# The first stage of a two-layer backbone step: a new order of steps, adaLN sums of two column blocks, weights and small vectors laid out by the host

## The chip, the cores and the metric

The kernel runs on one core of one Trainium2 chip. The metric is the device time of one launch in microseconds (us). Five engines work in parallel, each through its own instructions in order: TensorE (PE; its weight loads are listed apart as PEld), VectorE (DVE), ScalarE (ACT), GpSimd (POOL) and SyncE (SP), which here only issues DMA transfers. Engines wait for one another by semaphores.

## The reference

One inference step of a hybrid backbone with two layers, on 1024 latent ("sample") tokens and 256 context ("prompt") tokens of width 1024. What the first stage computes is the normalised and modulated input of layer 0, and the first of the projections behind it:

```
sh_p, sc_p, gt_p = _adaln(c_ctx[None, :], w_mod[l], b_mod[l])     # from silu(c) @ w_mod + b_mod
sh_s, sc_s, gt_s = _adaln(c, w_mod[l], b_mod[l])
hp = _rmsnorm(yp, norm_g[l]) * (1.0 + sc_p) + sh_p
hs = _rmsnorm(ys, norm_g[l]) * (1.0 + sc_s) + sh_s
...
qa, ka, va, za, qb, kb, vb, ob, zb, gb = jnp.split(h @ w_in, AB_SPLITS, axis=-1)
```

Layer 0 then runs windowed attention and a bidirectional matrix memory side by side, layer 1 latent attention; each ends in an output projection, a gate and a residual. All is float32 in and out. Products are made from pairs of rounded float32 parts, high and low, with three matmuls each (high by high, high by low, low by high).

## The kernel before

Tokens lie in three chunks: 0 and 1 of 512 sample tokens each, 2 of 256 prompt tokens. The input is ten tiles of 128 tokens by 1024, and the width is cut into KD = 8 column blocks k of 128.

The first stage is written out by hand: the text `STARTUP` is a list of steps, each a name with one or two digits, and `Startup.run` calls the method of that name. Each engine and each DMA queue gets its instructions in this order. No planner moves them. The steps are:

- `X t` loads token tile t (512 KB) and `W k i` a block of the adaLN weights: 1024 rows by 128 columns of the shift (i = 0) or the scale (i = 1), 512 KB, read in pieces of 512 B. Both take one of ten buffers `xin`. `F a` loads 256 rows by 256 columns of the first projection's weights into one of two buffers `wf` (256 KB). All go through SyncE's queue.
- `sq`, `xr`, `pw`, `sc`: sum of squares of a tile on ScalarE, its mean plus epsilon on VectorE, the power -0.5 on GpSimd, and the scaling of the tile by it (GpSimd for tiles 2, 4 and 6, VectorE for the others).
- `Ta`, `Tb`: four transposes each on TensorE; `ea`, `eb`: the copies out of PSUM into `xT` (ScalarE for a, VectorE for b).
- `M k`: the adaLN sums of column block k, 16 matmuls with the condition vectors as the stationary operand (32 records in the profile); `e`: their scaling by 0.5 on ScalarE; `C`: a transpose; `A`: four small VectorE operations, which leave the scale A and the shift B of block k.
- `t ci k`: xT times A plus B, on VectorE (line 370); `h`: its high part, on ScalarE (line 373); `l`: its low part, on VectorE or GpSimd (line 378).
- `c k`, `s k`: high part on ScalarE (line 362) and low part on GpSimd (line 366) of the projection's weights.
- `pa ci k`: for both units (two groups of 128 output columns) of chunk ci, the two products with the high part of the activations; `pb ci k`: the one with the low part. A wide product has 512 columns (chunks 0 and 1), a narrow one 256 (chunk 2). A unit adds up 24 of them in one PSUM bank, and then its `done` runs: a copy out of PSUM (line 1558), and a convolution over tokens with a gate (lines 1573 to 1583).

Ahead of the list, `setup_consts` and `setup_cond` load the constants and small vectors through ScalarE's queue; the vectors come as rows, and TensorE turns them into columns. Behind the list stand the loads (`after.ask`) and splits (`after.split`, lines 522 and 523) of the next block's weights, the block of attention values (272 columns, units of 24 matmuls for each tile of 128 tokens), and the products of chunk 2. The splits stand in the queues behind the convolutions, in this order:

```
after.ask()
after.ask()
for ci in range(2):
    start.pa(ci, KD - 1)
    start.pb(ci, KD - 1)
    after.split()
    after.ask()
for k in range(KD):
    start.pa(2, k)
    start.pb(2, k)
    if k in (1, 3):
        after.split()
```

After it come the values block, the gates of the matrix memory (a long chain of small VectorE operations, in `gates`) woven with the next projection, and all the rest.

Of the kernel before, what the change touches and what calls it, by code (L numbers as in the profile page):

```python
# [19 lines left out]
D = 1024  # L20
# [12 lines left out]
X0 X1 X2 sq0 X3 sq1 xr0 pw0 X4 sc0 sq2 xr1 Tb0 pw1 sq3 X5 xr2 Ta0 pw2 sc1 sc2 ea0 eb0 Tb1 W00 sq4 xr3  # L33
Ta1 eb1 pw3 Tb2 sq5 xr4 W01 sc3 pw4 Ta2 sc4 eb2 ea1 Tb3 X6 ea2 xr5 Ta3 eb3 ea3 pw5 Tb4 M0 X7 sc5 eb4 Ta4
e0 sq6 Tb5 W10 C0 eb5 Ta5 ea4 A0 W11 sq7 xr6 pw6 t00 sc6 ea5 F0 xr7 h00 W20 l00 pw7 M1 sc7 c1 W21 Tb6 c0
s1 Ta6 e1 eb6 Tb7 ea6 s0 Ta7 eb7 F1 C1 ea7 pb00 A1 W30 pa00 t10 M2 c3 t01 W31 c2 s3 h10 t11 s2 e2 pa10
h01 W40 l10 h11 C2 pa01 A2 W41 l01 M3 l11 t12 pa11 e3 F2 t02 h12 C3 X8 pb11 h02 l12 A3 M4 l02 c5 X9 pa02
c4 s5 t03 e4 C4 s4 t13 pa12 sq8 W50 pb02 A4 h03 pb10 xr8 t04 pw8 pb01 W51 sq9 pa03 l03 t14 h13 sc8 pb12
W60 h14 pa13 xr9 l13 pw9 h04 Tb8 l14 W61 sc9 M5 eb8 Tb9 e5 l04 F3 Ta9 C5 W70 ea9 eb9 Ta8 pb13 ea8 A5 M6
c7 W71 t23 c6 s7 pa04 t05 e6 h23 s6 t15 h05 C6 pb04 l23 A6 pa14 h15 l05 t25 M7 t16 h25 l25 pa15 t24 e7  # L40
h16 t06 C7 h24 pb05 l16 h06 A7 pa16 t22 pa06 l24 t07 h22 t17 l22 pb16 h07 pa05 t27 h17 l07 t20 pb14 h27
l17 pb03 h20 l27 t21 l20 t26 h21 l15 h26 l21 l06 l26 pb15 pb06
# [161 lines left out]
def setup_consts(K):  # L204
    nc, c = K.nc, K.const
    small = c.tile([128, 6, 128], F32, tag="small", name="small")
    K.dma_act(small, K.I["k_small"].rearrange("p (a f) -> p a f", a=6))
    K.small = small
    K.ident = small[:, 0, :]
    K.mbf = c.tile([128, 3, 128], BF16, tag="mbf", name="mbf")  # L210
    nc.vector.tensor_copy(K.mbf[:, 0, :], small[:, 0, :])
    nc.vector.tensor_copy(K.mbf[:, 1:3, :], small[:, 4:6, :])
# [9 lines left out]
def setup_cond(K, sp):  # L222
    nc, c = K.nc, K.const
    K.condT = c.tile([128, 16], F32, tag="condT", name="condT")
    crow = sp.tile([16, 128], F32, tag="crow", name="crow")
    cth = sp.tile([16, 128], F32, tag="cth", name="cth")
    K.dma_act(crow[0:8, :], K.I["c"].rearrange("a (k p) -> (a k) p", p=128))
    K.dma_act(crow[8:16, :], K.I["c_ctx"].rearrange("(k p) -> k p", p=128))
    nc.scalar.activation(cth, crow, AF.Tanh, scale=0.5)
    nc.vector.scalar_tensor_tensor(crow, cth, 1.0, crow, ALU.add, ALU.mult)  # L230
    ps = K.ps()
    K.tr(ps[:, 0:16], crow)
    nc.vector.tensor_copy(K.condT, ps[:, 0:16])

    grow = sp.tile([16, 128], F32, tag="grow", name="grow")
    K.dma_act(grow, K.I["norm_g"].rearrange("l (k p) -> (l k) p", p=128))
    K.gcol = c.tile([128, 16], F32, tag="gcol", name="gcol")
    ps = K.ps()
    K.tr(ps[:, 0:16], grow)
    nc.vector.tensor_copy(K.gcol, ps[:, 0:16])  # L240
    brow = sp.tile([16, 128], F32, tag="brow", name="brow")
    K.dma_act(brow, K.I["b_mod"][0, 0:2 * D].rearrange("(k p) -> k p", p=128))
    K.bcol = sp.tile([128, 16], F32, tag="bcol", name="bcol")
    ps = K.ps()
    K.tr(ps[:, 0:16], brow)
    nc.vector.tensor_copy(K.bcol[:, 0:8], ps[:, 0:8])
    nc.vector.tensor_scalar(K.bcol[:, 8:16], ps[:, 8:16], 1.0, None, ALU.add)
    cw = sp.tile([48, 128], F32, tag="cwr", name="cwr")
    K.dma_act(cw, K.I["conv_b"][0].rearrange("j (k p) -> (j k) p", p=128))
    K.cw = c.tile([128, 3, 16], F32, tag="cw", name="cw")  # L250
    ps = K.ps()
    K.tr(ps[:, 0:48], cw)
    pv = ps[:, 0:48].rearrange("p (j k) -> p j k", j=3)
    nc.vector.tensor_scalar(K.cw[:, :, 0:8], pv[:, :, 0:8], 0.5, None, ALU.mult)
    nc.vector.tensor_scalar(K.cw[:, :, 8:16], pv[:, :, 8:16], 1.0 / 32, None, ALU.mult)
    K.condP = cond_cols(K, sp)
    K.modd = [K.t(K.dram, [2, 3 * D], F32, f"modd{l}") for l in range(2)]
    K.A = [None, None]
    K.Bm = [None, None]


class Startup:


    def __init__(self, K, sp, first):
        self.K, self.sp, self.first = K, sp, first
        self.units = first.fn(first.w)
        first.w[:] = [None] * KD
        K.A[0], K.Bm[0] = [K.const.tile([128, 2, 8], F32, tag=f"{n}0", name=f"{n}0") for n in "AB"]
# [3 lines left out]
    def run(self, order):  # L273
        for token in order.split():
            name = token.rstrip("0123456789")
            getattr(self, name)(*[int(a) for a in token[len(name):]])
# [8 lines left out]
    def W(self, k, i):  # L285
        w = self.ws[k, i] = self.slot().rearrange("p (k f) -> p k f", k=KD)
        f = slice(i * D + k * 128, i * D + (k + 1) * 128)
        self.K.dma(w, self.K.I["w_mod"][0, :, f].rearrange("(k p) f -> p k f", p=128))

    def F(self, a):  # L290
        self.first.ask()
        self.wf[a] = self.first.wf.pop(0)

    def sq(self, t):
        ss = self.r[t] = self.K.t(self.sp, [128, 1], F32, "xss", 4)
# [3 lines left out]
    def xr(self, t):  # L299
        r = self.K.t(self.sp, [128, 1], F32, "xr", 4)  # L300
# [18 lines left out]
    def kept(self, t, a, copy):  # L319
        ci, i = chunk_of(t)  # L320
        copy(self.xT[ci][:, a:a + 4, i * 128:(i + 1) * 128], self.bank[t, a].rearrange("p (k t) -> p k t", k=4))
# [20 lines left out]
    def e(self, k):  # L342
        self.rows[k] = self.K.t(self.sp, [128, 128], F32, "mrow", 3)
        self.K.nc.scalar.mul(self.rows[k], self.bank[k][:, 0:128], 0.5)

    def C(self, k):
# [2119 lines left out]
```

## Time and profile before

| | |
|---|---|
| median of 3 runs | 2611.69 us (2610.7 to 2613.67) |
| the profiled execution's own time | 2613.18 us |
| its span, first to last instruction | 2611.4 us |
| mean granted TensorE clock | 0.992 |
| TensorE busy | 2541.8 us, 97% of the span |
| VectorE, ScalarE, GpSimd busy | 65%, 55%, 43% |
| first transposes of token tiles | 12.46 us |
| first product of the first block | 28.36 us |
| first matmul of the values block | 90.38 us |

The span is what the profile shows; the execution's own time has 1.8 us more around it. Of the rows shown further on: a row of instructions in order of time begins with its start and its duration, then engine, line, operation, tiles, shapes and count, and in brackets the idle time before it and what ended that. Rows of groups end with total busy time, mean duration in nanoseconds and the idle time before. A matmul's duration overlaps that of the next, so the pace is read from start to start. A row of waits has the total, the times and the longest.

### The profile page before, as it was taken

Reading aid. Unit: us, or ns where it says so; the run is one execution under the profiler, and the core shown is the slowest. Engines: PE = TensorE matmul, PEld = TensorE weight load, DVE = VectorE, ACT = ScalarE, POOL = GpSimd, SP = SyncE. Lnnn points to the kernel's source line nnn. Section 1 sums busy time; section 2 is a strip of 40 time slices with the busy share of each in tenths; the row PEclk is TensorE's granted clock in tenths of the full one; section 3 lists DMA queues with packets and bytes.
Section 4 is the critical chain, followed back from the end, with each engine's and each line's share of the span. In section 5 each row is a group of like instructions: output and inputs, shape, how many; then the busy total and the mean of one; then the engine's idle time right before and its main releaser. Section 6 shows DMA issues by size and latency. Waiting matters only on the chain.

```text
span 2611.4 us, 48697 instructions
## 1 busy us (share of the span) xinstructions
PE 2541.8 (97%) x16493; PEld 2253.4 (86%) x16493; DVE 1709.5 (65%) x3959; ACT 1438.4 (55%) x3660; POOL 1119.8 (43%) x1512
## 2 busy tenths in 40 slices
PE   7799999999999999999999999999999999999998
PEld 5789898898898888887888888898899999999887
DVE  7361565656647676577777546526888888888754
ACT  5332544544534433477666533234788888888842
POOL 5212333323224344356455453224455545555832
PEclk9899999999999999999999999999999999999999
DMA  8456576566666664445443454523311101101334
GB/s 242 154 177 187 164 198 194 163 199 188 176 200 207 211 212 145 140 145 154 134 124 109 131 192 134 159 73 101 87 32 32 44 27 38 36 27 30 119 99 131
DMA packets 352955, 347.21 MB, mean 133 GB/s; under 512 B 36065, under 2 KB 297886, under 8 KB 352450
## 3 DMA queue, kind: packets, MB, share of 16 engines
q1 hardware_dynamic: 352402, 343.65, 43.6%
q8 instruction: 131, 2.15, 0.4%
q14 instruction: 118, 0.97, 0.1%
q10 hardware_dynamic: 304, 0.44, 0.0%
HBM read 233.49 MB, written 110.50 MB: 132 GB/s over the span
## 4 chain that ended last, share of the span: by engine, by line
PE 84%; DVE 4%; DMA 4%; issue 3%; ACT 2%; POOL 2%; SPq 1%; ACTq 0%; POOLq 0%; DVEq 0%
PE mm L116 33%; PE S L116 29%; PE V L116 8%; PE T L120 6%; PE D L116 3%; PE mm L120 3%; SPq L151 1%; PE T L116 1%; DMA o_x<-y 1%; DMA att_q<-ql 0%; POOL wl L523 0%; DVE xT L370 0%; DMA caT<-csz 0%; POOL w L1022 0%; DMA w<-in_w_out_c 0%
## 5 line engine op out<-in xcount | busy, mean ns | idle before, releaser
L523 POOL TENSOR_TENSOR wl<-wf,wh 128x256 fp32r<-128x256 f32 (+3 forms) x280 | 223.4, 822 | 524.1 <-ACT wh L522 487.3
L116 PE MATMUL mm<-hTh,wh 128*128 128x512 f32 (+1 forms) x912 | 329.3, 361 | 0.9 <-DVE scr L769 0.9
L116 PE MATMUL mm<-hTl,wh 128*128 128x512 f32 (+1 forms) x912 | 324.6, 356 | 0.0
L116 PE MATMUL mm<-hTh,wl 128*128 128x512 f32 (+1 forms) x912 | 324.6, 356 | 0.0
L116 PE MATMUL S<-cK,cQ 96*128 96x512 f32 (+3 forms) x1248 | 301.0, 365 | 2.5 <-ACT cPa L2368 1.1
L2416 DVE TENSOR_TENSOR cpl<-T,cph 128x512 fp32r<-128x512 f32 x336 | 227.8, 685 | 38.2 <-ACT cph L2415 34.5
L116 PEld LDWEIGHTS S<-cK,cQ 96*128 96x128 f32 (+1 forms) x1248 | 192.6, 189 | 24.1 <-ACT cPa L2368 3.0
L2415 ACT CAST cph<-T 128x512 fp32r<-128x512 f32 x336 | 191.4, 589 | 29.1 <-PE T L120 16.8
L116 PEld LDWEIGHTS mm<-hTh,wl 128*128 128x128 f32 x912 | 171.4, 188 | 26.9
L116 PEld LDWEIGHTS mm<-hTh,wh 128*128 128x128 f32 x912 | 171.8, 188 | 23.9 <-DVE scr L769 1.1
L116 PEld LDWEIGHTS mm<-hTl,wh 128*128 128x128 f32 x912 | 171.9, 188 | 22.8
L2366 DVE TENSOR_REDUCE cmx<-S 128x1 f32<-128x512 f32 x256 | 173.2, 683 | 20.7 <-PE S L116 18.7
L116 PE MATMUL V<-cph,cV 128*128 128x256 f32 x672 | 177.1, 289 | 1.2 <-DVE co L2431 0.8
L116 PE MATMUL V<-cpl,cV 128*128 128x256 f32 x672 | 171.8, 284 | 0.8 <-DVE cst L2343 0.4
L1290 ACT CAST att_ph<-mm 128x512 fp32r<-128x512 f32 x168 | 98.5, 586 | 98.3 <-PE mm L120 96.5
L2347 POOL TENSOR_SCALAR cPa<-cPa,cst 128x512 f32<-128x512 f32 x128 | 98.7, 771 | 114.3 <-DVE cst L2344 93.3
L1291 DVE TENSOR_TENSOR att_pl<-mm,att_ph 128x512 fp32r<-128x512 f32 x168 | 115.8, 689 | 37.3 <-ACT att_ph L1290 32.1
L116 PE MATMUL mm<-wh,hTh 128*128 128x256 f32 x480 | 136.2, 284 | 4.1 <-DVE scr L1596 4.1
L116 PE MATMUL mm<-wl,hTh 128*128 128x256 f32 x480 | 135.4, 282 | 0.1
L116 PE MATMUL mm<-wh,hTl 128*128 128x256 f32 x480 | 135.3, 282 | 0.0
L116 PEld LDWEIGHTS V<-cph,cV 128*128 128x128 f32 x672 | 126.6, 188 | 8.3 <-DVE co L2431 1.4
L1279 POOL TENSOR_SCALAR att_p<-att_p,att_den 128x640 f32<-128x640 f32 (+1 forms) x128 | 97.4, 774 | 84.4 <-DVE att_den L1276 33.6
(472 smaller groups left out, 7772.1 us busy)
## 6 DMA issues: line engine op xcount, KB each, us to landing
wf<-in_w_in_ab SPq DMA_DIRECT2D x120, 256.0 KB
in<-in SPq DMA_DIRECT2D x40, 514.0 KB
in<-in SPq DMA_DIRECT2D x32, 386.0 KB
mw<-in_w_mod SPq DMA_DIRECT2D x48, 256.0 KB
in<-scr SPq DMA_DIRECT2D x40, 258.0 KB
o_x<-y SPq DMA_DIRECT2D x20, 512.0 KB
xin<-in_w_mod SPq DMA_DIRECT2D x16, 512.0 KB
in<-cx SPq DMA_DIRECT2D x32, 256.0 KB
```

The costliest lines, as they stand in the source:

```text
L116: return self.nc.tensor.matmul(out, lhsT, rhs, start=start, stop=stop)
L120: self.nc.tensor.transpose(out, in_, self.ident[:p, :p])
L151: self.nc.sync.dma_start(f(out), f(in_))
L523: K.nc.gpsimd.tensor_sub(wl, wf[:, k], wh.bitcast(F32))
L1279: nc.gpsimd.tensor_scalar(pv, pv, den[:, i:i + 1], 1.0, ALU.mult, ALU.mult)
L1290: K.nc.scalar.copy(ph, self.T)
L1291: K.nc.vector.tensor_sub(pl, self.T, ph.bitcast(F32))
L2347: nc.gpsimd.tensor_scalar(pv, pv, wt[:, c:c + 1], rd, ALU.mult, ALU.mult)
L2366: nc.vector.tensor_reduce(mx[:, b, c:c + 1], S, AX.X, ALU.max, negate=True)
L2415: nc.scalar.copy(ph, T_)
L2416: nc.vector.tensor_sub(pl, T_, ph.bitcast(F32))
```

## The change

- The list is new: 281 steps, with other orders of the tiles (6, 4, 2, 5, 3, 7, 0, 1, later 9 and 8) and of the column blocks. Steps that move or scale data have a letter for the engine: `a` ScalarE, `v` VectorE, `p` GpSimd (`ea4a`, `t13v`, `l01p`). The wide `t` run nine times on VectorE and seven on ScalarE, the narrow ones five and three times; the `l` run twelve times on VectorE and twelve on GpSimd; six tiles are scaled on GpSimd and four on VectorE; of the copies out of PSUM eleven run on ScalarE and nine on VectorE.
- `M q` sums column blocks 2q and 2q + 1 at once, from four W loads; `e`, `C` and `A` follow once for each q, and `A` has two VectorE operations.
- The host lays out `k_wmod` (16 blocks of 512 KB, one for each W, 4 KB in a row for each partition) and `k_cols` (the small vectors as columns). `LK` loads the constants and `LS` the columns, on SyncE's queue. `setup_cond`, with its loads on ScalarE's queue and its transposes, goes; three more small transposes behind the first stage go too.
- The list takes in what stood behind it: `f` (loads of the values block's weights), `d` (high parts, ScalarE), `u` (low parts), `P q` (the products of chunk 2 for two column blocks), `v ci j` (the copy out of PSUM of a unit of chunks 0 and 1) and `G` (buffers of the next stage). The convolutions run behind the list.
- One small ScalarE operation (`warm`) runs ahead of the list, and the buffers of the small vectors `xss` and `xr` go from 4 to 10.

```diff
 STARTUP = """
-X0 X1 X2 sq0 X3 sq1 xr0 pw0 X4 sc0 sq2 xr1 Tb0 pw1 sq3 X5 xr2 Ta0 pw2 sc1 sc2 ea0 eb0 Tb1 W00 sq4 xr3
...
-l17 pb03 h20 l27 t21 l20 t26 h21 l15 h26 l21 l06 l26 pb15 pb06
+X6 X4 X2 sq6 X5 sq4 xr6 pw6 X3 sc6p sq2 xr4 pw4 LK sq5 xr2 pw2 X7 sq3 xr5 sc4v pw5 LS Tb6 X0 sc5p sc2v Ta4
+eb6a Ta6 xr3 ea4a Tb2 X1 pw3 ea6v sq7 Tb5 eb2v sc3p Ta5 W10 Ta2 sq0 xr7 eb5v pw7 Tb3 W00 Tb4 sc7p sq1 xr0
+ea5v W11 pw0 Tb7 eb3a xr1 pw1 ea2a sc0v W01 cth Ta3 eb4a sc1v Ta7 eb7a Ta0 F0 ck ea3a Ta1 gc X9 ea7a ea0v M0
+W31 c0 ea1a e0v s0p C0 Tb0 W30 A0 sq9 Tb1 t00v W20 t10v h00 xr9 pa00 eb0v h10 W21 pw9 c1 l10v sc9p pa10 t11a
+X8 l00v t01a pb10 Tb9 h01 s1v F1 M1 h11 eb1v l01p W61 Ta9 e1v sq8 eb9v pb00 l11p W60 C1 pb01 A1 c2 pa11 c3
+xr8 W71 gw pw8 t02a s2v pb11 h02 pa01 sc8p t13v W70 ea9a t03v pa02 s3p h13 t12v F2 h03 Ta8 pa13 l02v ea8a F3
+l03p h12 W41 M3 t21v l13p t20v c5 pa12 t23a W50 l12v e3a c6 s5p C3 Tb8 c4 A3 W51 pa03 h23 s6p c7 t17v t07a
+pb03 s7p t06v W40 pb12 h07 pb02 t22v s4p h21 pb13 t16a eb8v pa07 l07p f0 h22 t27v h06 f1 M2 l22v h16 l06p
+t26a pb07 e2v h27 l21v C2 l23p h26 pa16 A2 h17 l26p t14v pa06 t25a t05a t04v l16p pb06 h14 pa17 t24v h05
+l17p l27v pa14 h20 l05v h04 pa05 h25 l04p t15a l25v pa04 l20v h15 l14v pb16 d3 l15p h24 pb05 d0 pb04 l24v d1
+pb14 u0v d2 pa15 G u3v v00 u2p u1v v01 pb17 f2 pb15 P0 f3 P1 d4 v11 u4p P2 d6 d5 d7 u5p v10 P3 u7v u6v
 """
...
     def W(self, k, i):
         w = self.ws[k, i] = self.slot().rearrange("p (k f) -> p k f", k=KD)
-        f = slice(i * D + k * 128, i * D + (k + 1) * 128)
-        self.K.dma(w, self.K.I["w_mod"][0, :, f].rearrange("(k p) f -> p k f", p=128))
+        self.K.dma(w, self.K.I["k_wmod"][i * KD + k].rearrange("p (k f) -> p k f", k=KD))
...
+    def M(self, q):
+        ps = self.bank[q] = self.K.psT()
         for j in range(KD):
             for i in range(2):
-                o = 64 * i + 32 * (j % 2)
-                self.K.mm(ps[o:o + 32, 0:128], self.K.condP[:, j, :], self.ws[k, i][:, j, :], j < 2, j >= KD - 2)
...
+                for k in range(2):
+                    o = 64 * i + 32 * k
+                    self.K.mm(ps[o:o + 32, 0:128], self.K.condP[:, j, :], self.ws[2 * q + k, i][:, j, :], j == 0, j == KD - 1)
...
+    def A(self, q):
+        nc, ks = self.K.nc, slice(2 * q, 2 * q + 2)
+        v = self.bank[q][:, 0:128].rearrange("p (i k r) -> p i k r", i=2, k=2)[:, :, :, 0:2]
+        b = self.cols[:, 32:48].rearrange("p (i k) -> p i k", i=2)[:, :, ks]
+        nc.vector.tensor_add(self.ab[:, :, ks], v, b.unsqueeze(3).to_broadcast([128, 2, 2, 2]))
+        a = self.ab[:, 1, ks]
+        nc.vector.tensor_mul(a, a, self.K.gcol[:, ks].unsqueeze(2).to_broadcast([128, 2, 2]))
...
+    def P(self, q):
+        for k in self.order[2 * q:2 * q + 2]:
+            self.pa(2, k)
+            self.pb(2, k)
+
+    def v(self, ci, j):
+        u = self.units[3 * j + ci]
+        u.done(u.ps)
+        self.kept.pop()()
...
     with K.tc.manual_schedule():
-        start.run(STARTUP)
...
-        for k in range(KD):
-            start.pa(2, k)
-            start.pb(2, k)
-            if k in (1, 3):
-                after.split()
+        start.run(STARTUP, room)
...
+def _layouts(inputs):
...
+    w = inputs["w_mod"][0, :, 0:2 * D].reshape(KD, 128, 2 * KD, 128)
+    return {"k_cols": np.ascontiguousarray(np.concatenate([a.reshape(-1, 128) for a in cols]).T),
+            "k_wmod": np.ascontiguousarray(w.transpose(2, 1, 0, 3)).reshape(2 * KD, 128, D)}
```

More of the change, by code (lines that the diff above doesn't have):

```diff
@@ L219, in setup_consts @@
     nc.vector.memset(K.mhalf, -0.5)
[L222 to L259, printed above, removed]
@@ L270, in __init__, with run @@
         self.x, self.r, self.ws, self.wf, self.bank, self.rows = {}, {}, {}, {}, {}, {}
         self.xT = [sp.tile([128, KD, N], F32, tag=f"xT{ci}", name=f"xT{ci}") for ci, (_, N) in enumerate(CHUNKS)]
-    def run(self, order):
-        for token in order.split():
-            name = token.rstrip("0123456789")
-            getattr(self, name)(*[int(a) for a in token[len(name):]])
+        warm = K.t(sp, [128, 1], F32, "warm", 1)
+        K.nc.scalar.activation(warm, K.mhalf, AF.Square)
+    def run(self, order, room):
+        K, nc = self.K, self.K.nc
+        self.G = room
+        self.by = dict(a=nc.scalar, v=nc.vector, p=nc.gpsimd)
+        K.flow = self
+        for token in order.split():
+            name, at, by = re.fullmatch(r"([A-Za-z]+)(\d*)([avp]?)", token).groups()
+            getattr(self, name)(*[int(a) for a in at], *by)
+        for u in self.units[2::3]:
+            u.done(u.ps)
+        while self.kept:
+            self.kept.pop(0)()
+        K.flow = None
+        small = K.small
+        nc.vector.tensor_copy(K.mbf[:, 0, :], small[:, 0, :])
+        nc.vector.tensor_copy(K.mbf[:, 1:3, :], small[:, 4:6, :])
@@ new lines, in later, with LK, LS, cth @@
+    def later(self, f, n):
+        self.kept.append(f)
+    def LK(self):
+        self.K.dma(self.K.small, self.K.I["k_small"].rearrange("p (a f) -> p a f", a=6))
+    def LS(self):
+        self.K.dma(self.cols, self.K.I["k_cols"][:, 0:96])
+    def cth(self):
+        self.th = self.K.t(self.sp, [128, 16], F32, "cth", 1)
+        self.K.nc.scalar.activation(self.th, self.cols[:, 0:16], AF.Tanh, scale=0.5)
+    def ck(self):
+        K = self.K
+        K.nc.vector.scalar_tensor_tensor(K.condT, self.th, 1.0, self.cols[:, 0:16], ALU.add, ALU.mult)
+        K.condP = cond_cols(K, self.sp)
@@ new lines, in cast, with low, s @@
+    def cast(self, b, k):
+        b.w[k] = [self.K.t(b.wp, [128, b.width], F32R, n, int(2 * b.bufs))[:, 0:sum(n for _, n in b.cols)] for n in ("wh", "wl")]
+        self.K.nc.scalar.copy(b.w[k][0], self.wf[b, k // 2][:, k % 2])
+    def low(self, b, k, by):
+        wh, wl = b.w[k]
+        self.by[by].tensor_sub(wl, self.wf[b, k // 2][:, k % 2], wh.bitcast(F32))
+    def c(self, k):
+        self.order.append(k)
+        self.cast(self.first, k)
+    def s(self, k, by):
+        self.low(self.first, k, by)
@@ L827, in layer_ab, with room @@
     dense = Dense(blocks)
-    start = Startup(K, sp, blocks.pop(0))
-    after = blocks[0]
-    K.set_psum(S=4, T=4)
-    with K.tc.manual_schedule():
-        start.run(STARTUP)
+    start = Startup(K, sp, blocks.pop(0), blocks[0])
+    def room():
+        nonlocal gp, tp
         sp.release()
@@ L836, in layer_ab @@
         K.cvp = right("conv")
-        after.ask()
-        after.ask()
-        for ci in range(2):
-            start.pa(ci, KD - 1)
-            start.pb(ci, KD - 1)
-            after.split()
-            after.ask()
-        for k in range(KD):
-            start.pa(2, k)
-            start.pb(2, k)
-            if k in (1, 3):
-                after.split()
+    gp = tp = None
+    K.set_psum(S=4, T=4)
+    with K.tc.manual_schedule():
+        start.run(STARTUP, room)
     K.set_psum(S=6, T=2)
```

160 lines of the change are left out of this document (81 added, 79 removed).

## The prediction

> **What bounds the kernel now.** I read the page first, for the span and the slices; then TensorE's waits in the first 131 us; then the busy time by stage; then the chain that ended last where the longest wait ends; last TensorE's instructions in order of time, for the price of one matmul of each kind. The page and the waits:
>
> ```profile
> span 2611.4 us, 48697 instructions
> ...
> PE   7799999999999999999999999999999999999998
> ```
>
> ```profile
> PE S L116 <- ACT scr L1558: 13.4, 1, 13.4
> ...
> PE S L116 <- DVE hTl L378: 3.3, 1, 3.3
> ```
>
> TensorE is busy nine tenths and more of nearly every slice; its free time lies in the first two slices, of 65 us each, and those are the stage that the change rewrites. By stage (length; busy time of TensorE, its weight loads, VectorE, ScalarE, GpSimd; granted clock, DMA share, GB/s):
>
> ```profile
> 0.00:12.46 12.46, 1.02 (x5) 0.67 (x5) 3.28 (x18) 5.97 (x10) 2.71 (x8) 1.00 0.88 318
> ...
> 28.36:58.70 30.34, 29.24 (x295) 22.23 (x294) 27.65 (x60) 17.34 (x39) 19.87 (x20) 0.96 0.81 223
> 58.70:75.50 16.80, 13.47 (x68) 10.68 (x67) 12.23 (x24) 6.10 (x14) 9.69 (x14) 0.80 0.50 160
> 75.50:90.40 14.90, 0.22 (x2) 0.16 (x2) 5.58 (x16) 5.20 (x13) 3.69 (x5) 0.61 0.39 103
> 90.40:120.40 30.00, 30.00 (x219) 30.00 (x220) 7.43 (x25) 6.52 (x18) 4.38 (x6) 0.91 0.34 110
> ```
>
> TensorE does almost nothing until 12.46, is full from 28.36 with VectorE nearly full beside it, and from 75.50 to 90.40 has 0.22 us of work in 14.90. The wait that ends this hole is put down to a ScalarE copy, so I follow the chain there (start, length, what):
>
> ```profile
> 83.51 1.37 ACT wh L522 x4
> ...
> 84.91 0.77 POOL wl L523
> ...
> 85.69 0.37 SPq L151
> ...
> 86.12 3.10 DMA wf<-in_w_in_ab
> ...
> 89.64 0.41 ACT wh L522
> ...
> 90.38 41.68 PE S L116 x333
> ```
>
> The hole is the next block's weights: four casts, which in ScalarE's order stood behind convolution work and ran only at 83.51, a GpSimd subtraction that frees a staging buffer, a load, the cast of that load, and then the first matmul of the block of attention values at 90.38. After it TensorE runs for 41.68 us without a break. So what counts is when that block can start; a microsecond that it comes earlier is carried on by TensorE, which is the bound from there to the end.
>
> **What one thing costs.** TensorE in order of time, start and duration first:
>
> ```profile
> 19.20 1.08 PE L116 MATMUL T<-xin,condP 128*32 128x128 f32 x32
> 20.21 1.09 PE L120 MATMUL T<-small,xin 128*128 128x128 f32 x8
> 21.14 0.27 PE L120 MATMUL T<-small,mrow 128*128 128x128 f32 x1
> ...
> 28.36 1.20 PE L116 MATMUL S<-hTl,wh 128*128 128x512 f32 x2
> ...
> 40.09 1.54 PE L116 MATMUL S<-hTl,wh 128*128 128x512 f32 x6
> 41.46 0.40 PE L116 MATMUL S<-hTh,wh 128*128 128x512 f32 x1
> ...
> 69.40 0.39 PE L116 MATMUL S<-hTh,wh 128*128 128x256 f32 x1
> ...
> 74.94 0.40 PE L116 MATMUL S<-hTl,wh 128*128 128x256 f32 x2
> ...
> 90.38 0.59 PE L116 MATMUL S<-wh,hTh 128*128 128x272 f32 x1 [13.35 <-ACT scr L1558]
> ...
> 95.30 0.43 PE L116 MATMUL S<-wh,hTh 128*128 128x272 f32 x1
> ...
> 96.13 0.29 PE L116 MATMUL S<-wh,hTl 128*128 128x272 f32 x1
> ...
> 99.03 0.28 PE L116 MATMUL S<-wl,hTh 128*128 128x272 f32 x1
> ```
>
> From start to start: one adaLN sum of a column block (M, 32 records) 20.21 - 19.20 = 1.01 us; eight transposes 0.93, 0.116 each; six 512-wide matmuls 41.46 - 40.09 = 1.37, 0.228 each; the matmuls of 256 columns 46 steps in 74.94 - 69.40 = 5.54, 0.120 each. So the first stage holds, at full clock, 80 transposes 9.3, eight M 8.1, 96 wide products 21.9, 48 narrow ones 5.8 and some 0.4 of small transposes: 45.5 us.
>
> **The change, part by part.** Small vectors from the host: the six loads that ScalarE issued and four transposes with their copies go, and three more in the stages behind; one load of the columns (48 KB) and the constants go through SyncE's queue instead, ahead of the last X tiles. They add 0.44 MB there. The removed transposes lay before TensorE had anything else, or in the hole: nothing of their own.
>
> One M for two column blocks: as many matmuls (four times 64 records for eight times 32), while the scalings, transposes and the small VectorE work after them halve. That relieves VectorE, and makes a group of four W loads the unit that TensorE waits for.
>
> The adaLN weights' layout: each of the 16 W loads is one block of 4 KB a partition, as the X loads are, no longer 512 B pieces. The rate of X shows early, that of W with some F late:
>
> ```profile
> 7.00:12.00 5.00, 1.02 (x4) 0.64 (x4) 2.24 (x9) 4.93 (x9) 1.75 (x3) 1.00 1.03 379
> ...
> 42.00:47.00 5.00, 3.90 (x50) 3.02 (x49) 4.55 (x6) 2.02 (x6) 3.12 (x3) 1.00 0.97 264
> ```
>
> No run shows W in the new form. The ends are these rates, 379 and 264 GB/s, at a DMA share near 1.0 both times; I take 379, because the new form is that of X. The Trainium skill ("DMA: Bandwidth & Descriptors", Specifications) puts line rate at transfers of 512 B and more, by which W was there already and the layout would bring nothing. These rows, 264 in 512 B pieces beside 379, speak against it; the first rival is what it would make of the time.
>
> The order. Up to the first M the queue holds eight X, four W, constants and columns, 6.73 MB; with transfers from about 2 us on (the first row of the stage table: 318 GB/s over 12.46 us is 3.96 MB, 10.45 us at 379), they have landed at 2 + 6.73/0.379 = 19.8. M0 now sums two blocks, 2.0 us, to 21.8. Before, a first product took from 19.20 to 28.36, because other transposes stood in between; the chain itself is scaling, transpose, A, t and h:
>
> ```profile
> 20.37 0.28 ACT L344 ACTIVATE mrow<-T 128x128 f32<-128x128 f32 x1 [1.28 <-PE T L116]
> ...
> 23.57 0.63 ACT L373 CAST hTh<-xT 128x512 fp32r<-128x512 f32 x1
> ```
>
> ```profile
> 22.13 0.22 DVE L355 SCALAR_TENSOR_TENSOR B<-T,bcol,mhalf 128x2 f32<-128x2 f32 x1
> ...
> 22.78 0.56 DVE L370 TENSOR_SCALAR xT<-xT,A,B 128x512 f32<-128x512 f32 x1
> ...
> 29.46 3.37 DVE L370 TENSOR_SCALAR xT<-xT,A,B 128x512 f32<-128x512 f32 x3
> ```
>
> 0.3 for the scaling, 0.3 for the transpose, two VectorE operations 0.4, t 0.6, h 0.6, and 0.5 for the hand-overs: 2.7, so a first product at 24.5, 3.9 us earlier. Done by then are the transposes of eight X tiles (64, 7.4 us), M0 (2.0) and 0.1: 36.0 us of TensorE work are left, and the stage's last matmul would end at 60.5 if nothing stalled. What does stalling cost? Before, the work from 28.36 on was 96 wide and 48 narrow products, seven M, 17 transposes and the small ones, 21.9 + 5.8 + 7.1 + 2.0 + 0.8 = 37.6 us, and took 75.2 - 28.36 = 46.8: 9.2 lost, to the 3.3 us wait and to clocks of 0.96 and 0.80 above all. The new order's loss lies between 0 and 9.2; below 0 it can't go, as the work is counted at full clock. I take half, 4.6, since VectorE, which was nearly full, gives work away (nine wide t's for 16, five narrow for eight, six wide l's for eight, A's 32 operations become eight) and gets six narrow l's for none and five low parts of the next block, while ScalarE takes ten t's and eight casts. ScalarE has room for them:
>
> ```profile
> L297 ACT ACTIVATE xjk<-xin 128x1024 bf16<-128x1024 f32 x10 | 10.6, 1055 | 1.2 <-DMA xin<-in_x_prompt 1.1
> L373 ACT CAST hTh<-xT 128x512 fp32r<-128x512 f32 x16 | 9.4, 617 | 1.4 <-DVE xT L370 1.4
> L321 ACT COPY xT<-T 128x512 f32<-128x512 f32 x10 | 5.7, 582 | 7.1 <-PE T L120 7.1
> L373 ACT CAST hTh<-xT 128x256 fp32r<-128x256 f32 x8 | 3.2, 405 | 5.2 <-DVE xT L370 5.1
> L362 ACT CAST wh<-wf 128x256 fp32r<-128x256 f32 x8 | 2.9, 409 | 0.5 <-DMA wf<-in_w_in_ab 0.5
> ```
>
> squares 10.6, h's 9.4 and 3.2, eleven copies 6.4, ten t's at h's prices 5.5, 16 casts 6.5: 42 us in about 60. GpSimd does 12 l's for 16, six scalings for three and nine low parts for eight, so about what it did. Neither exceeds TensorE. The stage's last matmul then ends at 60.5 + 4.6 = 65.1.
>
> The check by DMA: up to the last W the queue holds 26 blocks of 0.524 MB, four F of 0.262, and the 0.44: 15.1 MB, landed at 2 + 15.1/0.379 = 41.8. M2, the last to run, ends near 43.8, and the list has behind it seven pa (four wide matmuls each), eight pb (two) and P0 to P3: 44 at 0.228 and 5.8, together 15.8, so 59.6 at the earliest. The transfers set nothing as long as the higher rate holds. In SyncE's queue W41 stands behind F3, whose staging buffer is free only after the first pair of splits; the four W ahead of it are then still under way.
>
> The next block's weights (f, d, u) move from behind the convolutions into the list; casts and subtractions, eight of each, are paid either way. Late are f2 and f3, which need the u's of the first pairs: a load 3.10, a cast 0.4, a subtraction 0.8, covered by P0 to P3 (5.8) and the block's first half unit. I put the hand-over at 0.5; its bounds are 0 and the 13.35 of before. The convolutions that ran in the hole go behind, beside a stretch where VectorE needs 7.43 of 30.00. The v steps put ScalarE copies ahead of P0; were they late, P0 would wait for banks, which the stalls' bounds take in.
>
> So the values block starts at 65.6, not at 90.38: 24.8 us. And its first 21 steps, from 90.38 to 95.30, took 0.234 each where (99.03 - 96.13)/23 = 0.126 was the pace later: without the hole the clock is not lost, 21 x 0.108 = 2.3. Sum: 27.1 us.
>
> **Against which time.** The profiled execution took 2613.18 for a span of 2611.4; it stands 1.5 above the median of the runs, 2611.69. 2613.18 - 27.1 = 2586.1; against the median 2584.6, which I round to 2585.
>
> **The rivals.** First, W goes no faster than before. Then the X part lands at 2 + 4.63/0.379 = 14.2, the other 10.5 MB at 0.264 in 39.8, to 54.0; M2 and the 15.8 behind it end at 71.8, with a microsecond of lower clock and the hand-over 73.3, and the gain is 90.4 - 73.3 + 2.3 = 19.4: 2592. For it: the DMA share is full at 264; against it: X at 379 in the same share. It is what the rule of the Trainium skill named above would give.
>
> Second, the tail opens a hole of its own: f3's trip of load, cast and subtraction, 4.7 us like that from 85.69 to 90.38, stays uncovered, the clock is lost again behind it (2.3), and stalls are at the upper end (9.2 for 4.6): 27.1 - 4.7 - 2.3 - 4.6 = 15.5, 2596.
>
> Third, no change: the block starts early, but the wait comes back in the gates' VectorE chain behind it, as long as the whole 27 us: 2611. The convolutions pushed behind would have to fill the 22.6 us that VectorE has free there first; I give it little.
>
> Fourth, slower: the W blocks are read at a rate below both. The gain is gone if the stage's last matmul ends after 92, so if W lands after 74, which is 10.5 MB in 60 us, 175 GB/s; at 150 it lands at 84 and the time is 2621. X tiles are such blocks and went at 379: very unlikely.
>
> **How the numbers follow.** The forecast with its stalls of 0 to 9.2 (2580 to 2590) has 0.60, a gain beyond it 0.06, W slow 0.12, the tail 0.14, no change 0.04, slower 0.04. This kernel's measurement tells about 0.2%, 5 us, from nothing. The range 2577 to 2598 leaves out no change, slower and the ends of tail and gain, some 0.15. Faster 0.92, same 0.04, slower 0.04.
>
> **What would show it.** In the changed profile: DMA of 350 GB/s or more until about 42; a first wide product at 24 to 25; M2 at 42 to 46; the last 256-column product at 61 to 69; no wait of over 2 us ahead of the values block, and its matmuls at 0.126 from the first; the stretch behind it as long as before. I am wrong if W shows 270 GB/s, if VectorE's t's beside a busy GpSimd (0.56 alone at 22.78, 1.12 each at 29.46) hold TensorE up by more than 9 us, or if the gates' stretch grows a hole.

## The result, and the profile after

| | before | after |
|---|---|---|
| median of the runs compared | 2611.19 us (2610.46 to 2613.67, 4 runs) | 2592.29 us (2588.86 to 2594.18, 4 runs) |
| ratio, with its 95% interval | | 0.9924 [0.9907, 0.9942] |
| the profiled execution's own time, span | 2613.18, 2611.4 us | 2588.86, 2587.1 us |
| start of the values block | 90.38 us | 68.20 us |
| first product of the next stage (tile `mm`) | 230.11 us | 207.81 us |

The change saves 18.9 us between the medians, where the prediction said 26.7 (2611.69 to 2585); the time lies inside the predicted range. Line numbers differ in the changed kernel: the matmuls are line 118 and the transposes 122 (116 and 120 before), the copy of a unit out of PSUM 1586 (1558), the convolution's multiply 1601 and its tanh 1607 (1573 and 1579), the casts of weights 390, h 414, l 418.

The page of the changed kernel, its span and TensorE's slices:

```profile
span 2587.1 us, 48628 instructions
...
PE   7999999999999999999999999999999999999998
```

TensorE's waits in its first 131 us (total, times, longest):

```profile
PE S L118 <- ACT scr L1586: 3.2, 1, 3.2
PE S L118 <- ACT hTh L414: 1.6, 2, 0.9
...
PE T L118 <- DMA xin<-in_k_wmod: 0.7, 2, 0.4
PE S L118 <- DVE hTl L418: 0.6, 1, 0.6
```

The 13.4 us and the 3.3 us of before are gone; one wait of 3.2 is left, put down to the same kind of copy. By stage (length; busy time of TensorE, weight loads, VectorE, ScalarE, GpSimd; granted clock, DMA share, GB/s):

```profile
25.87:45.12 19.25, 18.66 (x199) 14.69 (x199) 16.30 (x28) 14.97 (x31) 15.94 (x14) 1.00 0.89 334
45.12:65.02 19.90, 18.61 (x157) 15.50 (x157) 12.93 (x30) 11.67 (x27) 13.82 (x17) 1.00 0.36 96
65.02:68.20 3.18, 0.00 (x0) 0.00 (x1) 2.70 (x12) 3.18 (x7) 0.44 (x1) 1.00 1.00 364
68.20:98.20 30.00, 30.00 (x227) 30.00 (x228) 15.47 (x42) 9.67 (x24) 3.96 (x5) 0.94 0.53 153
```

The first products run from 25.87 to 65.02 at full clock with 1.9 us of free time in all (19.25 - 18.66 + 19.90 - 18.61), where before VectorE was the partner that TensorE waited for; VectorE now has 16.30 of 19.25 and then 12.93 of 19.90. Then comes a hole of 3.18 us in which TensorE has no work and ScalarE is never idle. TensorE in order of time (start, duration, what; idle time before it):

```profile
25.87 0.50 PE L118 MATMUL S<-hTh,wh 128*128 128x512 f32 x1 [0.90 <-ACT hTh L414]
...
45.12 1.95 PE L118 MATMUL T<-xin,condP 128*32 128x128 f32 x64 [0.42 <-DMA xin<-in_k_wmod]
...
64.62 0.40 PE L118 MATMUL S<-hTl,wh 128*128 128x256 f32 x2
68.20 0.39 PE L118 MATMUL S<-wh,hTh 128*128 128x272 f32 x1 [3.18 <-ACT scr L1586]
...
69.57 0.43 PE L118 MATMUL S<-wl,hTh 128*128 128x272 f32 x1
...
72.96 0.29 PE L118 MATMUL S<-wl,hTh 128*128 128x272 f32 x1
```

and ScalarE around the hole:

```profile
63.89 1.06 ACT L390 CAST wh<-wf 128x272 fp32r<-128x272 f32 x3 [1.58 <-DMA wf<-in_w_in_ab]
64.86 0.58 ACT L1586 COPY scr<-S 128x512 f32<-128x512 f32 x1
65.33 2.56 ACT L1601 ACTIVATE cx<-scr,cw 128x512 f32<-128x512 f32 x4
67.79 0.62 ACT L1586 COPY scr<-S 128x256 f32<-128x256 f32 x2
```

Read them together: the weights are there (the last casts ended at 64.95, the last low part, on VectorE, at 66.40), but ScalarE, whose casts had stood 1.58 us for the block's last load, does the four multiplies of the convolutions that were put off, 2.56 us, and only then chunk 2's two copies at 67.79; TensorE goes on once the first of them has been made. By this reading the values block's first sum waits for a PSUM bank, not for weights; the second experiment tests it.

### The profile page after: what moved, and what is told of

It reads as the page before. It is cut to its first block, busy times and chain, and to the rows that moved or that the text cites. A ratio compares the mean times of both kernels' runs of the same rounds, so it can differ in the third digit from the quotient of the medians.

```text
span 2587.1 us, 48628 instructions
## 1 busy us (share of the span) xinstructions
PE 2534.7 (98%) x16482; PEld 2250.6 (87%) x16482; DVE 1694.8 (66%) x3932; ACT 1442.1 (56%) x3665; POOL 1111.0 (43%) x1504
## 5 line engine op out<-in xcount | busy, mean ns | idle before, releaser
L569 POOL TENSOR_TENSOR wl<-wf,wh 128x256 fp32r<-128x256 f32 (+2 forms) x272 | 216.8, 822 | 511.4 <-ACT wh L568 445.6
```

The lines of the kernel that those rows point to most:

```text
L569: K.nc.gpsimd.tensor_sub(wl, wf[:, k], wh.bitcast(F32))
```

## The experiments

Each ratio is to the runs of the kernel before on the same chip (their medians 2610.97, 2610.66 and 2611.33 in the three sets). "Start" is the first matmul of the values block, the first with a 272-column operand.

| kernel | time, us | ratio [95%] | start, us | wait ahead of it, us |
|---|---|---|---|---|
| before | 2611.19 | 1 | 90.38 | 13.35 |
| after | 2592.29 | 0.9924 [0.9907, 0.9942] | 68.20 | 3.18 |
| after, once more | 2591.56 | 0.9928 [0.9915, 0.9941] | 68.11 | 3.61 |
| copies first | 2586.88 | 0.9908 [0.9895, 0.9921] | 67.48 | 1.22 |
| copies first, once more | 2586.59 | 0.9901 [0.9886, 0.9917] | 67.71 | 1.19 |
| copies first, other banks | 2586.48 | 0.9907 [0.9895, 0.9920] | 66.78 | 0.99 |
| after, W in 512 B pieces | 2594.00 | 0.9935 [0.9923, 0.9946] | 73.81 | 3.87 |
| after, without the steps `f`, `d`, `u` | 2588.51 | 0.9916 [0.9902, 0.9929] | 67.04 | 0.35 |
| after, convolutions in place | 2595.92 | 0.9941 [0.9929, 0.9954] | 76.96 | 11.37 |
| after, engines as before | 2592.34 | 0.9930 [0.9917, 0.9942] | 71.14 | 4.34 |
| copies first, F3 behind W | 2587.02 | 0.9906 [0.9893, 0.9920] | 69.94 | 1.12 |
| before, tail alone | 2596.94 | 0.9947 [0.9934, 0.9961] | 75.68 | 0.40 |
| before, W layout alone | 2610.66 | 0.9997 [0.9988, 1.0006] | 90.4 | 13.6 |

**The changed kernel once more**, unedited.

> The changed kernel once more, unedited, for the spread and for a second trace. If the gain of some 22 us that the first stage shows is what counts, the median lies 19 to 24 us under the kernel before, and two traces of it agree at 200 us to 0.5 us and differ only in the stages behind 1000 us. If instead the changed kernel's stages behind the first are slower by themselves, both traces show the same later stage longer.

It repeats the result: 2591.56, and the same hole (3.61 us). The two traces were to agree within 0.5 us at 200 us, and they don't: the next stage's first product comes at 206.30 for 207.81. Nearly all of these 1.5 us lies in the stretch of the gates, where the first trace lost clock and this one did not (shown further down).

**Is the hole made by the order on ScalarE?** Chunk 2's copies go ahead of the put-off convolutions:

```diff
+        first = self.kept[:]
+        self.kept = []
         for u in self.units[2::3]:
             u.done(u.ps)
+            self.kept.pop()()
+        last, self.kept = self.kept, []
+        for f in first:
+            f()
+        self.kept += last
```

> Behind the list the copies out of PSUM of chunk 2's two sums run ahead of the four convolution multiplies (0.64 us each on ScalarE), nothing else changed. Theory: the 3.2 us wait ahead of the values block is this order on ScalarE, as the block's first sum needs a bank that these copies free; then the wait falls to 1 us or so, the block starts at 66 and not 68.2, and with the lower clock behind the wait (14 steps of 0.1 us) gone the kernel gains 2 to 3.6 us on the changed one. Rival: the wait is for the block's own weights (f3, d7, u6, u7); then the start stays at 68 and the time is the same.

> The kernel with the copies of chunk 2 ahead of the put-off convolutions once more, for the comparison on this chip. Theory: as before, 2585 to 2588, values block from 66.8 to 68, no wait over 1.5 us between the stage's last product and the values block.

ScalarE of the second of these two runs, and TensorE's first matmul of the values block:

```profile
65.84 1.06 ACT L397 CAST wh<-wf 128x272 fp32r<-128x272 f32 x3 [2.00 <-DMA wf<-in_w_in_ab]
66.81 1.12 ACT L1593 COPY scr<-S 128x512 f32<-128x512 f32 x3
67.81 2.57 ACT L1608 ACTIVATE cx<-scr,cw 128x512 f32<-128x512 f32 x4
```

```profile
46.85 1.96 PE L118 MATMUL T<-xin,condP 128*32 128x128 f32 x64 [1.55 <-DMA xin<-in_k_wmod]
...
67.71 0.40 PE L118 MATMUL S<-wh,hTh 128*128 128x272 f32 x1 [1.19 <-ACT scr L1593]
```

The multiplies now stand behind the copies, the wait is 1.2 us, and in both runs the matmuls behind it keep the full clock. The start was forecast at 66, and it is 67.48 and 67.71, only 0.4 to 0.7 us earlier than in the changed kernel: in both traces M2 began later (46.36 and 46.85 for 45.12 and 44.93), after a longer wait for W (1.34 and 1.55 us for 0.42 and 0.75). The edit stands behind M2 in every queue, so by the kernel's text this is not its doing; why W came later stays open. Counted from M2 to the start, the traces have 21.12 and 20.86 us for 23.08 and 23.18, 2.0 to 2.3 us less. To that comes the clock, 1.5 us (14 slow steps of 0.1). The medians fall by 4.7 us in the same set (2591.56 to 2586.88). The two intervals just overlap, but all three sets with the copies first lie at 2586.5 to 2586.9 and both of the changed kernel at 2591.6 to 2592.3. That most of the hole is the order on ScalarE is shown; the 1.2 us that are left stand behind casts that waited 2.0 and 2.1 us for the block's last load. These are the shortest times found.

**A free bank instead of an early copy.** The same kernel with the PSUM pools of the next stage given out the other way round, so that its first sum falls on other banks:

```diff
-    K.set_psum(S=6, T=2)
+    K.set_psum(T=2, S=6)
```

> As the run with the copies first, and the values block's banks begin with two that were free earlier (the pool of the two transpose banks is laid out first). Theory of the banks: the wait goes almost wholly, start at 65 to 65.5, another 0.5 to 1 us. Rival (weights late): start at 68 as before, no gain; if the last low parts (u7, u6) are the next thing to be late, a short wait appears after the first half unit instead.

The wait does not go: 0.99 us are left, now put down to a VectorE operation, where almost nothing was forecast. The start is 0.7 to 0.9 us earlier, but M2 also began 0.6 to 1.1 us earlier (45.77), and the time is the same (2586.48). Once the copies come first, the choice of banks gains nothing that can be measured.

**The layout of W.** The changed kernel with W read in pieces of 512 B, as before:

```diff
-        self.K.dma(w, self.K.I["k_wmod"][i * KD + k].rearrange("p (k f) -> p k f", k=KD))
+        f = slice(i * D + k * 128, i * D + (k + 1) * 128)
+        self.K.dma(w, self.K.I["w_mod"][0, :, f].rearrange("(k p) f -> p k f", p=128))
```

> The changed kernel with the 16 W loads read from the original weights again, in 512 B pieces. Theory: W goes at 264 to 310 GB/s for 400, M2 starts at 51 to 54 for 45, the stage's last matmul comes 5 to 8 us later (70 to 73), and the time is 5 to 8 us over the changed kernel. Rival, by which 512 B pieces run at line rate: W at 390 or more, no difference.

and the kernel before with W laid out by the host, nothing else:

> The kernel before with the host's layout of the W blocks alone. Theory: the loads end some 8 us earlier, but the old order on VectorE sets that stage's pace, so of it 0 to 4 us arrive at the end. Rival (the transfers bound the old stage): 6 us or more. By the rule that 512 B pieces already run at line rate: nothing, and no rate over 310 GB/s in the W windows.

The rates while W is under way, first the changed kernel, then the same with 512 B pieces (length; busy times; clock, DMA share, GB/s):

```profile
27.00:32.00 5.00, 4.84 (x81) 3.79 (x80) 3.13 (x6) 3.97 (x8) 4.10 (x3) 1.00 1.03 404
```

```profile
27.00:32.00 5.00, 3.56 (x18) 2.36 (x18) 3.79 (x7) 3.65 (x7) 4.48 (x4) 1.00 1.12 319
...
42.00:47.00 5.00, 5.00 (x66) 4.17 (x58) 3.09 (x7) 4.37 (x11) 3.62 (x5) 1.00 1.13 296
```

and TensorE's wait for W with 512 B pieces:

```profile
PE T L118 <- DMA xin<-in_w_mod: 4.8, 4, 1.6
```

So in these windows the DMA moves 404 GB/s with W in blocks of 4 KB a partition, and 296 to 319 with W in 512 B pieces, with the DMA engines fully busy both times. In the new order each of the four sums then waits, 4.8 us in all, and the values block starts 5.7 us later (73.81 for 68.11). In time that is 2594.00 beside 2591.56, and the two intervals overlap: the 5.7 us are seen in the trace, not in the medians, where 5 to 8 us were forecast. In the old order the same layout brings nothing, 0.9997: W is read faster there too (404 GB/s from 36 to 41 us, where before has 320), but the waits that held the first stage, for VectorE and for the copy behind the convolutions, are those of before:

```profile
PE S L116 <- ACT scr L1557: 13.6, 1, 13.6
...
PE S L116 <- DVE hTl L377: 3.4, 1, 3.4
```

**Is it the early loads and splits that closed the old hole?** The changed kernel without the steps `f`, `d` and `u`; the convolutions stay put off. The edit takes these 20 steps out of `STARTUP`, so that the block's own loads and splits, which stand behind the list in the program, do this work. In `Startup.__init__`

```diff
-        first.w[:], after.w[:] = [None] * KD, [None] * KD
+        first.w[:] = [None] * KD
```

> The changed kernel without the steps f, d and u: the values block's weights are loaded and split behind the list and the convolutions, as in the kernel before. Theory (the old hole came from these splits standing behind convolution work): a hole of 6 to 13 us opens ahead of the values block, with 2 us of lower clock behind it, and the time is 6 to 13 us over the changed kernel. Rival (the hole came from the small vectors' loads and transposes, which are gone either way): no more than 2 us.

The hole does not come back, it is smaller than ever (0.35 us). But this is no test of late loads and splits. The order fixed by hand ends with the list, and what stands behind it in the program did not run behind it. SyncE's queue in this run, then the changed kernel's rows for its last two loads (f2 and f3):

```profile
41.33 13.64 SPq L154 DMA_DIRECT2D wf<-in_w_in_ab  x8
```

```profile
58.29 0.89 SPq L153 DMA_DIRECT2D wf<-in_w_in_ab  x2
...
59.80 0.88 SPq L153 DMA_DIRECT2D wf<-in_w_in_ab  x2
```

All loads of the values block (two transfers for each of the four) are issued between 41.33 and 54.97; the changed kernel issues the last two at 58.29 and 59.80. ScalarE in this run:

```profile
46.79 0.74 ACT L569 CAST wh<-wf 128x272 fp32r<-128x272 f32 x2 [0.73 <-DMA wf<-in_w_in_ab]
...
48.26 0.73 ACT L569 CAST wh<-wf 128x272 fp32r<-128x272 f32 x2
...
61.08 1.08 ACT L1587 COPY scr<-S 128x512 f32<-128x512 f32 x2 [2.90 <-PE S L119]
62.04 1.96 ACT L1602 ACTIVATE cx<-scr,cw 128x512 f32<-128x512 f32 x3
63.89 0.41 ACT L569 CAST wh<-wf 128x272 fp32r<-128x272 f32 x1
64.20 0.73 ACT L1602 ACTIVATE cx<-scr,cw 128x512 f32<-128x512 f32 x1
64.82 1.05 ACT L569 CAST wh<-wf 128x272 fp32r<-128x272 f32 x3
66.61 0.65 ACT L1587 COPY scr<-S 128x256 f32<-128x256 f32 x2 [0.74 <-PE S L119]
```

Half of the casts run at 46.79 to 48.99, where the changed kernel's first run at 54.62. No cast stands still for the last load, so the multiplies begin at 62.04, beside chunk 2's products, and not at 65.33 behind them, and the copies are on time. A part of the short wait is only that the last product came later (66.69 for 65.02). So the run shows the other half of the hole of 3.18 us, a last load that came too late for the queue it stood in; whether late splits would bring the old hole back, it doesn't say. The next run put the convolutions back where they were.

**Convolutions in place**, with loads and splits in the list as the change has them:

```diff
     def v(self, ci, j):
         u = self.units[3 * j + ci]
         u.done(u.ps)
-        self.kept.pop()()
+        while self.kept:
+            self.kept.pop(0)()
```

> The changed kernel, with each convolution run in full where its unit is copied out (steps v11 and v10), as before the change, and not put off behind the list. Loads and splits of the values block's weights stay in the list. Theory (the hole of 13.4 us was ScalarE's queue standing at the convolutions' tanh, each of which waits 1.6 to 2.8 us for VectorE's taps, with the weights' casts and chunk 2's copies behind; what took it away is the putting off): ScalarE stands at the tanh again, four of them with 8 us of waits in all before, four multiplies and four tanh of 2.6 each take 5 us beside; d4 to d7 and chunk 2's copies come that much later, the values block starts at 72 to 76 where the changed kernel has 68.2 and the one with the copies first 67.5, and the longest wait ahead of it is 6 to 10 us; the time is 2594 to 2600. Rival (the early loads and splits in the list took the hole away, the convolutions' place matters little): start at 67 to 69, no wait over 3.5 us, time 2587 to 2592.

Now the hole is back, 11.37 us, a little longer than the 6 to 10 that were forecast, and the start is at 76.96. ScalarE in it, and TensorE:

```profile
65.02 0.63 ACT L1608 ACTIVATE scr<-cx 128x512 f32<-128x512 f32 x1 [0.99 <-DVE cx L1606]
...
71.78 0.63 ACT L1608 ACTIVATE scr<-cx 128x512 f32<-128x512 f32 x1 [2.02 <-DVE cx L1606]
...
76.02 0.63 ACT L1608 ACTIVATE scr<-cx 128x512 f32<-128x512 f32 x1 [1.07 <-DVE cx L1606]
76.56 0.63 ACT L1587 COPY scr<-S 128x256 f32<-128x256 f32 x2
```

```profile
76.96 0.60 PE L118 MATMUL S<-wh,hTh 128*128 128x272 f32 x1 [11.37 <-ACT scr L1587]
```

Line 1608 is the convolution's tanh, which needs two VectorE operations first; ScalarE stands at it four times, and chunk 2's copies stand behind the last. A part of the last one's lateness comes from VectorE's own queue, which stood 2.63 us at a small load (`m`, a row at 75.04) ahead of the convolution's second operation. The kernel before shows the same rows at 71.93 to 82.98:

```profile
71.93 0.63 ACT L1579 ACTIVATE scr<-cx 128x512 f32<-128x512 f32 x1 [1.61 <-DVE cx L1577]
...
82.98 0.63 ACT L1579 ACTIVATE scr<-cx 128x512 f32<-128x512 f32 x1 [2.83 <-DVE cx L1577]
83.51 1.36 ACT L522 CAST wh<-wf 128x272 fp32r<-128x272 f32 x4
```

Wait ahead of the values block with the convolutions in place: 13.35 us in the old list with splits behind them, 11.37 in the new list with splits in it. With the convolutions put off: 3.18 in the new list, 0.35 with the loads issued earlier still. In the same list, then, with the same loads and splits, the place of the convolutions alone makes 11.37 us of 3.18. The early splits are not enough to close the hole while chunk 2's copies stand behind the tanh. How much they add once the convolutions are put off no run shows, for none has them late and the convolutions behind.

**The tail alone.** The kernel before, with the splits ahead of the last products and the convolutions put off, the list and its engines as they were (the class `Keep` keeps what a convolution would run later):

```diff
+        K.flow = keep = Keep()
...
+        for _ in range(2):
+            after.split()
+            after.ask()
         for ci in range(2):
...
-            after.split()
-            after.ask()
         for k in range(KD):
...
-            if k in (1, 3):
+            if k in (3, 5):
                 after.split()
+        K.flow = None
+        keep.run()
```

> The kernel before with one part of the change: the values block's weights are split ahead of the convolutions, which wait until chunk 2's products are issued; list, loads and small vectors are the old ones. Theory: the hole of 13.35 us shrinks to 1 to 4, the clock behind it is kept; 10 to 14 us under the kernel before, about half of the change's gain, the list giving the other half. Rival (the list and the early start are the gain): under 3 us.

2596.94, so 13.7 us come with the tail alone, in the old first stage: some 70% of the 18.9 us of the whole change, where about half was forecast.

```profile
75.68 0.39 PE L116 MATMUL S<-wh,hTh 128*128 128x272 f32 x1 [0.40 <-ACT scr L1578]
```

The new list, the engines, the layout and the small vectors together add 5 to 6 us to that in the changed kernel, where a part of what they gain is lost again in the hole of 3.18 us, and 10 to 12 with the copies first. The small vectors and the sums of two column blocks were not tried alone.

**The order with the old engines.** The changed kernel with its list, but each step's letter set to the engine that the kernel before gave that work:

> The changed kernel's order with the engines of the kernel before (45 of the steps get another letter: all t on VectorE, copies a on ScalarE and b on VectorE, the l of chunk 2 on GpSimd, scalings, s and u as before). Theory: VectorE and GpSimd bound the stage again, its last matmul comes 4 to 9 us later than 64.9 and the time is 4 to 9 us over the changed kernel. Rival (the order alone carries it): within 2 us.

My theory fell: the time is that of the changed kernel (2592.34 for 2591.56 and 2592.29), and the last product comes 1.8 us later than there (66.80 for 65.02), not 4 to 9. The start is 3 us later in the trace (71.14), which the times can't tell. So of what the list gains, the new engines give 3 us at most.

**Is F3 in the way?** SyncE's queue of the changed kernel (start, how long the queue's instructions took, what):

```profile
24.50 3.16 SPq L153 DMA_DIRECT2D xin<-in_k_wmod  x4
28.92 7.58 SPq L153 DMA_DIRECT2D wf<-in_w_in_ab  x2
36.59 1.89 SPq L153 DMA_DIRECT2D xin<-in_k_wmod  x4
```

The queue stands 7.58 us at F2 and F3, whose staging buffer is not free, and the last four W start only at 36.59. The DMA engines run half empty meanwhile (and from 35 to 37, at 31 GB/s, nearly so):

```profile
34.00:36.00 2.00, 2.00 (x11) 1.57 (x10) 2.00 (x3) 1.78 (x4) 2.00 (x2) 1.00 0.51 175
```

So these four W were put ahead of F3, in the kernel with the copies first:

```diff
-... Ta8 pa13 l02v ea8a F3
-l03p h12 W41 M3 ... t23a W50 l12v ... A3 W51 pa03 ... t06v W40 pb12
+... Ta8 pa13 l02v ea8a W41
+W50 W51 W40 F3 l03p h12 M3 ... t23a l12v ... A3 pa03 ... t06v pb12
```

> The kernel with the copies of chunk 2 ahead of the put-off convolutions, and the last four loads of the adaLN weights ahead of F3 in SyncE's queue, where F3 stood 7.6 us for its buffer. Theory (the queue's stand at F3, not the rate, made the last W late): the four W are issued at about 32 and landed by 39, where they landed at about 45; the wait of 0.4 to 1.7 us ahead of M2 is gone, M2 still starts by its place in the list at 44 to 45, the values block starts 1 to 1.5 us earlier than with the copies first alone (66 to 66.5 for 67.5); time 2585 to 2587. Rival (F3, now behind four W, comes late for its cast): TensorE waits 1 us or more for h or wh around 40 to 48 and the start is no earlier than 67.5.

The rival was right. The W are issued at 31.63, but F3 lands later, and the cast of its weights holds ScalarE, with the h behind it:

```profile
43.66 0.71 ACT L397 CAST wh<-wf 128x256 fp32r<-128x256 f32 x2 [3.40 <-DMA wf<-in_w_in_ab]
```

```profile
46.41 0.50 PE L118 MATMUL S<-hTh,wh 128*128 128x512 f32 x1 [2.02 <-ACT hTh L421]
```

The start is 2.2 us later than with the copies first alone (69.94 for 67.71), the time the same. F3's place costs 0.4 and 0.75 us at M2 in the changed kernel's two traces and up to 1.55 with the copies first, and it can't simply be moved.

## Why the prediction was right, and where its sum was off

The direction and the range held, and so did the main of the mechanism: the values block starts 22.2 us earlier, and TensorE carries it on. What ends the old hole was put down to the wrong part, and the hand-over was mis-sized. Point by point:

- **W at 379 GB/s: right, a little low.** 404 in the new form, 296 to 319 in the old one in the same order. The rule of the Trainium skill ("DMA: Bandwidth & Descriptors", Specifications), line rate from 512 B on, does not hold for these reads: the 512 B pieces stay a quarter below. The first rival, 2592 by that rule, names the measured time only by chance; its mechanism is not there. With 512 B pieces the start is late by 5.7 us, where it had 7.7 (73.3 for 65.6). The sign "350 GB/s or more until about 42" failed at the stand of F2 and F3 (31 GB/s from 35 to 37).
- **Where the layout gains.** By the trace, the stage's end moves from 75.3 to 69.9 by the rest of the change (512 B pieces) and to 65.0 with the layout: some 5 us each. In the old order the layout is worth nothing, as the run of it alone shows: a transfer that is not the bound gives nothing until another change makes it the bound.
- **The last W at 41.8: wrong.** M2 began only at 45.12, with a wait for W. The prediction saw the place, W41 behind F3, and said that the four W ahead would still be under way; but the queue stood until 36.5, and the rate fell to 175 GB/s from 34 and to 31 from 35 on. It cost 0.4 us in this trace, since M2 stands that late in the list anyway.
- **First product at 24.5, loss 4.6, end at 65.1: the end was right, the parts were not.** The first product came at 25.87, mostly because the weights for the first sum landed later (TensorE waits for them until 21.35, where the sum has 19.8); from there the 36.0 us of work took until 65.02, 3.1 us lost. The two errors cancel.
- **The hand-over at 0.5: this is the term that was mis-sized.** It measured 3.18 us. The prediction looked for a late weight (f2, f3) and found cover for it on TensorE; what came late was a PSUM bank. On ScalarE the cast of f3's weights stood 1.58 us for its load, with four multiplies of the put-off convolutions behind it, and chunk 2's copies behind those. It counted the convolutions as going "beside a stretch where VectorE needs 7.43 of 30.00" and left out ScalarE, where they stand ahead of chunk 2's copies. The bounds (0 to 13.35) held it.
- **The clock's 2.3 us: only a part of it came.** The prediction had the matmuls at 0.126 from the first; behind the hole they ran at full clock until 69.57 and then at 0.227 until 72.96, so the 25 steps from 68.20 took 4.76 us instead of 3.15: 1.6 of the 2.3 lost again. In the kernels with the copies first nothing is lost there.
- **Early loads and splits as what ends the old hole: not enough.** The prediction named the convolution work as a part of the chain, but put the gain down to the steps f, d and u. With these steps and the convolutions in place the hole is still 11.37 us, and its end is chunk 2's copy behind the tanh, not a weight. That the convolutions go behind, which the prediction had as a side effect, is what the gain needs. What the early splits add to it stays open.
- **"No wait of over 2 us ahead of the values block"** was therefore wrong by the same 3.18 us; "the stretch behind as long as before" was right to 0.1 us up to the next stage's first product, by two effects that cancel in this pair of traces. In the stretch behind, the gates' hole stays what it was, but here it costs the clock (first before, then after, then after once more):

```profile
158.37 0.78 PE L120 MATMUL T<-small,LI 36*128 36x36 f32 x10 [2.56 <-DVE scr L1560]
```

```profile
135.25 1.25 PE L122 MATMUL T<-small,LI 36*128 36x36 f32 x10 [2.78 <-DVE scr L1588]
```

```profile
135.06 0.78 PE L122 MATMUL T<-small,LI 36*128 36x36 f32 x10 [2.68 <-DVE scr L1588]
```

In the second row the same ten transposes take 1.25 us for 0.78, and the matmuls after them run at 0.212 for 0.117 until 141.26. The next stage's first products, at 230.11 and 207.81, are 22.3 us apart, like the starts of the values block (22.2): what the full clock there gained, the gates' stretch gave back. In the third row, the same kernel, it did not, and that product comes at 206.30, 23.8 us earlier than before. So the 0.1 us is luck of the pair.

So of the 27.1 us of the sum, 22.3 stand in the trace; 2.6 are missing at the start of the values block (68.20 for 65.6), nearly all of it the hand-over, and the clock's 2.3 did not stay in this trace (1.5 of it did in the second). From that product to the end of the span the profiled executions differ by 2.0 (2381.3 before, 2379.3 after), so the profiled pair differs by 24.3, the medians by 18.9. The profiled execution of after is the fastest of its four runs and that of before (2613.18) stands near the slowest of its own; over the kernels of this study this rest took 2378.4 to 2385.6 us, in no relation to what had been edited. What makes this scatter stays open; it is as large as the smaller effects here, which is why they are given from the trace and not from the medians. With the copies first, the kernel takes 2586.6 to 2586.9, within 2 us of the predicted 2585; that is close by chance too, for its start of 67.5 to 67.7 is still 2 us late.

## What to carry to other kernels

When work is pushed behind another stage to free the engine that waits, look at every in-order queue it now stands in: here the weights were there, but on ScalarE a cast that waited for its load and four multiplies stood ahead of two copies that free PSUM banks, and TensorE lost 3.2 us and some 1.5 of clock behind them. An operation in a queue costs its neighbours what it waits for as well as what it does: of a chain that goes to and fro between two engines, let only the part that waits for nothing run ahead, and put off the rest. A faster transfer pays only where the transfer is the bound; tried alone in the old order it showed nothing, in the new order some 5 us in the trace.

## What the runs showed of the hardware

- **A short wait can cost the clock, and its length alone does not tell.** After waits of 0.35 to 1.22 us ahead of the values block (six traces) the matmuls ran at 0.126 us from the second step on. After 3.18 to 4.34 us (the changed kernel twice, 512 B pieces, old engines) 14 or 15 steps ran at 0.227 instead, about 1.5 us lost. They need not start with the first matmul: in the changed kernel they start 1.4 us after it, 4.6 us after the wait began, with the old engines right behind it. At the gates waits of 2.56 to 2.78 us, and one of 3.39, cost the clock in nine of the 13 traces and nothing in four, and the same kernel did both: the changed one lost it after 2.78 us and kept it after 2.68, the one with the copies first kept it after 2.68 and lost it after 2.67. The slow stretches keep a beat of their own: in each of the six traces that have two or more of them (the kernel before, the same with the W layout, after, convolutions in place, old engines, tail alone) their ends lie 27.3, 68.1 to 68.3 or 78.7 us apart, which is 8, 20 and 23 times 3.41 within 0.2. In the changed kernel they are 72.96 and 141.07 to 141.26. The Trainium skill ("TensorE: Matmul & The Clock Gate", Part 1) has a free-running window of about 3.4 us, one idle window of which halves the clock and one busy window of which restores it, and its rule from this is to leave no gap of more than about 3.4 us. The beat, the slow stretch of 3.4 us (69.57 to 72.96) and the nearly doubled step agree with the window and the halving; as a rule for gaps 3.4 us is too long here, for waits of 2.57 to 3.18 us were enough. That the place of a wait within the window decides at 2.6 us would follow from this; it is argued, not tested.
- **DMA.** Windows with W in 4 KB a partition reached 404 GB/s, with W in 512 B pieces 296 to 319, at a DMA share that is higher for the slower ones (1.12 to 1.13 for 1.03): the share shows that the engines are occupied, not that they are at their best.
